# A softmax with quarter rows on each partition, two DMA queues and another order of the vector work

## The chip, the cores and the metric

The kernel runs on one core of a Trainium2 chip. The core has a vector engine (VectorE, DVE in the profile), a scalar engine (ScalarE, ACT), GpSimd (POOL), TensorE (PE, not used here) and SyncE (SP), which only issues DMA transfers and waits. All transfers between the chip's main memory (HBM) and the on-chip memory (SBUF, 128 partitions) run on 16 DMA engines. The metric is the device time of one execution in microseconds; lower is better. Three runs of the kernel before gave 2492.26, 2494.18 and 2495.42 us, so the median is 2494.18 us.

## The reference

The input is `logits`, 16 x 256 x 32768 values of float32, and a temperature of 1.0. Each of the 4096 rows gets a softmax over its 32768 values:

```python
scaled = logits / temperature
scaled = scaled - scaled.max(axis=-1, keepdims=True)
exp_scaled = np.exp(scaled)
return (exp_scaled / exp_scaled.sum(axis=-1, keepdims=True)).astype(np.float32)
```

The input has 536.87 MB and so has the output. Every value is read once and written once.

## The kernel before

A row is cut into two halves of 16384 values, and each half lies on one partition (`_SPLIT = 2`), so two neighbouring partitions hold one row. The 8192 half rows make 64 groups (`G`) of 128 partitions. A group is cut along the row into two chunks of 8192 values (`_CW`, `C = 2`): a chunk is a buffer of 128 x 8192 float32, 32 KB on each partition and 4 MiB in all. There are six such buffers (`_BUFS`), in a pool whose tiles are handed out in turn, and 128 chunks.

For each chunk, `exps` (L94) takes the negative maximum of the chunk on VectorE (L107) and then the exponential in place on ScalarE with that maximum as bias (L114), which adds up the sum of the exponentials as it goes. So each chunk has a maximum of its own. When both chunks of a group are through, `factors` (L123) brings them together: the smaller of the two negative maxima (L129), the same across the two partitions of a row by a shuffle and a combination (`combine`, L84 and L87), the correction of each chunk's maximum (L131, on ScalarE), the corrected sum (L138), again a shuffle and a combination, the reciprocal (L149) and a factor for each chunk (L150). This block has high priority in the scheduler. `scales` (L152) then multiplies a chunk by its factor: the first 4096 values of each partition on VectorE (L160), the other 4096 on ScalarE (L163). In the last group the pieces are 4096 values long.

All transfers are issued on SyncE's queue, loads at L64 and stores at L75, each in the order of the program (`keep_in_program_order`). That order is the list at L170: six loads first, store 0, and from then on store i followed by load i + 5. A load waits until the store that empties its buffer has landed; a store waits for both scaling instructions. The transfers of the first group's loads and of all of the last group are cut into two of 2 MiB. The order of the compute instructions on each engine is left to the scheduler.

Of the kernel before, what the change touches and what calls it, by code (L numbers as in the profile page):

```python
# [6 lines left out]


_SPLIT = 2
_CW = 8192  # L10
_BUFS = 6
_PIECE = 8192
_LAST_DMA = 4096
_DVE_SHARE = 0.5


@with_exitstack
def kernel(
    ctx: ExitStack,
    tc: tile.TileContext,  # L20
    logits: bass.AP,
    temperature: bass.AP,
    out: bass.AP,
):
    nc = tc.nc
    inv_t = 1.0 / float(temperature)
    P = nc.NUM_PARTITIONS
    fp32 = mybir.dt.float32
    Exp = mybir.ActivationFunctionType.Exp
    Copy = mybir.ActivationFunctionType.Copy  # L30
    X = mybir.AxisListType.X
    A = mybir.AluOpType

    xf = logits.flatten_outer_dims()
    of = out.flatten_outer_dims()
    N, V = xf.shape
    W = V // _SPLIT
    CW = min(_CW, W)
    C = W // CW
    assert W * _SPLIT == V and CW * C == W and (N * _SPLIT) % P == 0  # L40
    x = xf.rearrange("n (h v) -> (n h) v", h=_SPLIT)
    o = of.rearrange("n (h v) -> (n h) v", h=_SPLIT)
    G = N * _SPLIT // P
    n_chunks = G * C
    n_rounds = _SPLIT.bit_length() - 1

    xpool = ctx.enter_context(tc.tile_pool(name="x", bufs=_BUFS))
    spool = ctx.enter_context(tc.tile_pool(name="stats", bufs=3))
    slots = {}
    stats = {}  # L50

    def spans(total: int, step: int) -> list[tuple[int, int]]:
        return [(s, min(step, total - s)) for s in range(0, total, step)]

    def piece(g: int) -> int:
        return _PIECE if g < G - 1 else min(_PIECE, _LAST_DMA)

    def load(i: int) -> None:
        g, c = divmod(i, C)
        xs = xpool.tile([P, CW], fp32, tag="x", name="xs")  # L60
        slots[i] = xs
        for s, n in spans(CW, _LAST_DMA if g in (0, G - 1) else CW):
            tc.keep_in_program_order(
                nc.sync.dma_start(  # L64
                    out=xs[:, s : s + n],
                    in_=x[g * P : (g + 1) * P, c * CW + s : c * CW + s + n],
                )
            )

    def store(i: int) -> None:  # L70
        g, c = divmod(i, C)
        xs = slots.pop(i)
        for s, n in spans(CW, _LAST_DMA if g == G - 1 else CW):
            tc.keep_in_program_order(
                nc.sync.dma_start(  # L75
                    out=o[g * P : (g + 1) * P, c * CW + s : c * CW + s + n],
                    in_=xs[:, s : s + n],
                )
            )

    def combine(v, op) -> None:
        for j in range(n_rounds):
            mask = [i ^ (1 << j) for i in range(32)]
            nc.vector.stream_shuffle(  # L84
                out=v[:, j + 1 : j + 2], in_=v[:, j : j + 1], mask=mask
            )
            nc.vector.tensor_tensor(  # L87
                out=v[:, j + 1 : j + 2],
                in0=v[:, j : j + 1],
                in1=v[:, j + 1 : j + 2],  # L90
                op=op,
            )

    def exps(i: int) -> None:  # L94
        g, c = divmod(i, C)
        xs = slots[i]
        ps = spans(CW, piece(g))
        K = C * len(ps)
        if c == 0:
            stats[g] = tuple(  # L100
                spool.tile([P, K], fp32, tag=f"{nm}{K}", name=nm)
                for nm in ("nm", "ssum", "ee", "f", "ttj")
            )
        nm, ssum = stats[g][:2]
        for j, (s, n) in enumerate(ps):
            k = c * len(ps) + j
            nc.vector.tensor_reduce(  # L107
                out=nm[:, k : k + 1], in_=xs[:, s : s + n], axis=X, op=A.max, negate=True
            )
            if inv_t != 1.0:  # L110
                nc.vector.tensor_scalar_mul(
                    out=nm[:, k : k + 1], in0=nm[:, k : k + 1], scalar1=inv_t
                )
            nc.scalar.activation(  # L114
                out=xs[:, s : s + n],
                in_=xs[:, s : s + n],
                func=Exp,
                bias=nm[:, k : k + 1],
                scale=inv_t,
                accum_out=ssum[:, k : k + 1],  # L120
            )

    def factors(g: int) -> None:  # L123
        nm, ssum, ee, f, ttj = stats[g]
        nMh = spool.tile([P, 1 + n_rounds], fp32, tag="nMh", name="nMh")
        Sh = spool.tile([P, 1 + n_rounds], fp32, tag="Sh", name="Sh")
        rS = spool.tile([P, 1], fp32, tag="rS", name="rS")
        with tc.high_priority():
            nc.vector.tensor_reduce(out=nMh[:, 0:1], in_=nm, axis=X, op=A.min)  # L129
            combine(nMh, A.min)  # L130
            nc.scalar.activation(  # L131
                out=ee,
                in_=nm,
                func=Exp,
                bias=nMh[:, n_rounds : n_rounds + 1],
                scale=-1.0,
            )
            nc.vector.tensor_tensor_reduce(  # L138
                out=ttj,
                in0=ee,  # L140
                in1=ssum,
                scale=1.0,
                scalar=0.0,
                op0=A.mult,
                op1=A.add,
                accum_out=Sh[:, 0:1],
            )
            combine(Sh, A.add)
            nc.vector.reciprocal(out=rS, in_=Sh[:, n_rounds : n_rounds + 1])  # L149
            nc.vector.tensor_scalar_mul(out=f, in0=ee, scalar1=rS)  # L150

    def scales(i: int) -> None:  # L152
        g, c = divmod(i, C)
        xs = slots[i]
        f = stats[g][3]
        ps = spans(CW, piece(g))
        for j, (s, n) in enumerate(ps):
            k = c * len(ps) + j
            cut = int(n * _DVE_SHARE) // 512 * 512
            nc.vector.tensor_scalar_mul(  # L160
                out=xs[:, s : s + cut], in0=xs[:, s : s + cut], scalar1=f[:, k : k + 1]
            )
            nc.scalar.activation(  # L163
                out=xs[:, s + cut : s + n],
                in_=xs[:, s + cut : s + n],
                func=Copy,
                scale=f[:, k : k + 1],
            )

    order = [("L", i) for i in range(min(_BUFS, n_chunks))] + [("S", 0)]  # L170
    for i in range(1, n_chunks):
        order.append(("S", i))
        if i + _BUFS - 1 < n_chunks:
            order.append(("L", i + _BUFS - 1))

    nxt = 0
    done = -1
    loaded = 0
    for kind, i in order:
        if kind == "L":  # L180
            load(i)
            loaded = i + 1
        else:
            g = i // C
            if g > done:
                while nxt < (g + 1) * C:
                    assert nxt < loaded
                    exps(nxt)
                    nxt += 1
                factors(g)  # L190
                done = g
            scales(i)
            store(i)


# [33 lines left out]
```

## Time and profile before

| what | value |
|---|---|
| median of three runs | 2494.18 us |
| span of the profiled execution | 2493.8 us |
| VectorE busy | 1487.4 us (60%) |
| ScalarE busy | 1405.0 us (56%) |
| HBM read and written | 536.87 MB each |
| mean rate over the span | 431 GB/s |
| load, issue to landing (4096 KB) | 29.0 us |
| store, issue to landing (4096 KB) | 38.2 us |

The profiled execution has no time of its own beside its span; the span lies 0.4 us under the median of the runs. The page gives the busy time of each engine, the DMA engines' share and rate in slices of the span, the DMA queues, the chain of work that ended last, and the costliest groups of instructions. Such a group is a line of the kernel, an engine and an operation with its shapes; then come the busy time in all, the mean of one in ns, and the idle time of the engine before them with what ended it. A line of a stretch of time gives the stretch, its length, the busy time of DVE, ACT and POOL with their instruction counts, the granted TensorE clock, the share of time that the DMA engines were busy, and GB/s.

### The profile page before, as it was taken

The page shows a single profiled execution, that of the slowest core. Times are in us where ns is not written, and L with a number is a line of the kernel's source. Part 1 is how long each engine was busy: PE and PEld are TensorE (multiplying, and loading weights), DVE is VectorE, ACT ScalarE, POOL GpSimd, SP SyncE. Part 2 cuts the span into 40 slices and gives each one's busy share as a digit, 9 for nine tenths or more (in the row PEclk, how much of TensorE's full clock was granted, in tenths as well). Part 3 has the DMA queues.
Part 4 walks back from the last instruction along what each step waited for, and adds up shares of the span by engine and source line. Part 5 has one row for each costly group of instructions (what it writes and reads, how often), then busy time and mean ns, then how long its engine had stood idle before and what let it go on. Part 6 is the DMA issues. An engine that isn't in the chain of part 4 may idle for free.

```text
span 2493.8 us, 2234 instructions
## 1 busy us (share of the span) xinstructions
DVE 1487.4 (60%) x964; ACT 1405.0 (56%) x455; POOL 0.2 (0%) x4
## 2 busy tenths in 40 slices
DVE  7655565556655566555665566655666566655663
ACT  5665554655556555565555655555546555465553
POOL 0000000000000000000000000000000000000000
DMA  9999999999999999999999999999999999999998
GB/s 412 433 430 432 429 431 432 433 433 434 433 434 432 435 432 435 432 435 431 436 431 435 432 434 433 434 433 433 433 433 433 433 433 434 434 433 434 432 431 368
DMA packets 37745, 1073.90 MB, mean 431 GB/s; under 512 B 4192, under 2 KB 4192, under 8 KB 4192
## 3 DMA queue, kind: packets, MB, share of 16 engines
q1 hardware_dynamic: 37728, 1073.76, 99.9%
q14 instruction: 17, 0.14, 0.0%
HBM read 536.87 MB, written 536.87 MB: 431 GB/s over the span
## 4 chain that ended last, share of the span: by engine, by line
DMA 96%; SPq 1%; ACT 1%; DVE 1%; issue 1%; ACTq 0%
DMA out_dram<-xs 93%; DMA xs<-in_logits_dram 2%; SPq L64 1%; DVE nm L107 1%; ACT xs L163 1%; ACT xs L114 0%; ACTq L224 0%; SPq L75 0%; DVE f L150 0%; ACT ee L131 0%; DVE rS L149 0%; DVE Sh L87 0%; DVE ttj L138 0%; DVE Sh L84 0%; DVE Sh L138 0%
## 5 line engine op out<-in xcount | busy, mean ns | idle before, releaser
L114 ACT ACTIVATE xs<-xs,nm 128x8192 f32<-128x8192 f32 (+1 forms) x130 | 912.1, 7016 | 972.4 <-DVE nm L107 972.4
L107 DVE TENSOR_REDUCE nm<-xs 128x1 f32<-128x8192 f32 (+1 forms) x130 | 1111.6, 8551 | 527.3 <-DMA xs<-in_logits_dram 527.3
L163 ACT ACTIVATE xs<-xs,f 128x4096 f32<-128x4096 f32 (+1 forms) x130 | 468.1, 3648 | 71.4 <-DVE f L150 71.4
L160 DVE TENSOR_SCALAR xs<-xs,f 128x4096 f32<-128x4096 f32 (+1 forms) x130 | 295.7, 2318 | 3.7 <-DVE f L150 1.8
L138 DVE CUSTOM_DVE_ANT_0 ttj<-ee,ssum 128x2 f32<-128x2 f32 x64 | 10.3, 161 | 423.8 <-ACT ee L131 423.8
L114 ACT ACTIVATION_READ_ACCUMULATOR xs<-xs,nm 128x1 f32 x130 | 24.2, 186 | 0.0
L131 ACT ACTIVATE ee<-nm,nMh 128x2 f32<-128x2 f32 x64 | 17.9, 280 | 0.0
L150 DVE TENSOR_SCALAR f<-ee,rS 128x2 f32<-128x2 f32 x64 | 14.6, 229 | 2.2
L149 DVE RECIPROCAL rS<-Sh 128x1 f32<-128x1 f32 x64 | 10.5, 164 | 2.2
L87 DVE TENSOR_TENSOR nMh<-nMh 128x1 f32<-128x1 f32 x64 | 10.2, 160 | 2.2
L87 DVE TENSOR_TENSOR Sh<-Sh 128x1 f32<-128x1 f32 x64 | 10.2, 160 | 2.2
L129 DVE TENSOR_REDUCE nMh<-nm 128x1 f32<-128x2 f32 x64 | 9.9, 155 | 2.2
L84 DVE STREAM_SHUFFLE nMh<-nMh 128x1 f32<-128x1 f32 x64 | 9.7, 151 | 0.0
L84 DVE STREAM_SHUFFLE Sh<-Sh 128x1 f32<-128x1 f32 x64 | 9.7, 151 | 0.0
L114 ACT ACT_TABLE_LOAD x1 | 1.3, 1283 | 12.9 <-DMA xs<-in_logits_dram 12.9
L138 DVE DVE_READ_ACCUMULATOR2_ANT Sh<- 128x1 f32 x64 | 5.3, 84 | 0.0
L84 DVE LOAD_MASK_SELECT Sh<-Sh x64 | 0.9, 14 | 2.8
L84 DVE LOAD_MASK_SELECT nMh<-nMh x64 | 0.9, 14 | 2.7
L210 POOL MEMSET const-bfloat16-1.0<- 128x1 bf16 x1 | 0.1, 102 | 0.0
L210 POOL MEMSET const-uint8-127<- 128x1 uint8 x1 | 0.1, 102 | 0.0
L210 POOL MEMSET const-float32-0.0<- 128x1 f32 x1 | 0.1, 99 | 0.2 <-issue 0.2
L210 POOL MEMSET const-float32-1.0<- 128x1 f32 x1 | 0.1, 99 | 0.0
## 6 DMA issues: line engine op xcount, KB each, us to landing
out_dram<-xs SPq DMA_DIRECT2D x126, 4096.0 KB, 38.2
xs<-in_logits_dram SPq DMA_DIRECT2D x124, 4096.0 KB, 29.0
xs<-in_logits_dram SPq DMA_DIRECT2D x8, 2048.0 KB, 22.3
out_dram<-xs SPq DMA_DIRECT2D x4, 2048.0 KB, 26.7
```

Source lines behind the costliest of these rows:

```text
L64: nc.sync.dma_start(out=xs[:, s : s + n], in_=x[g * P : (g + 1) * P, c * CW + s : c * CW + s + n],)
L84: nc.vector.stream_shuffle(out=v[:, j + 1 : j + 2], in_=v[:, j : j + 1], mask=mask)
L87: nc.vector.tensor_tensor(out=v[:, j + 1 : j + 2], in0=v[:, j : j + 1], in1=v[:, j + 1 : j + 2], op=op,)
L107: nc.vector.tensor_reduce(out=nm[:, k : k + 1], in_=xs[:, s : s + n], axis=X, op=A.max, negate=True)
L114: nc.scalar.activation(out=xs[:, s : s + n], in_=xs[:, s : s + n], func=Exp, bias=nm[:, k : k + 1], scale=inv_t, accum_out=ssum[:, k : k + 1],
L129: nc.vector.tensor_reduce(out=nMh[:, 0:1], in_=nm, axis=X, op=A.min)
L131: nc.scalar.activation(out=ee, in_=nm, func=Exp, bias=nMh[:, n_rounds : n_rounds + 1], scale=-1.0,)
L138: nc.vector.tensor_tensor_reduce(out=ttj, in0=ee, in1=ssum, scale=1.0, scalar=0.0, op0=A.mult, op1=A.add, accum_out=Sh[:, 0:1],)
L149: nc.vector.reciprocal(out=rS, in_=Sh[:, n_rounds : n_rounds + 1])
L150: nc.vector.tensor_scalar_mul(out=f, in0=ee, scalar1=rS)
L160: nc.vector.tensor_scalar_mul(out=xs[:, s : s + cut], in0=xs[:, s : s + cut], scalar1=f[:, k : k + 1])
L163: nc.scalar.activation(out=xs[:, s + cut : s + n], in_=xs[:, s + cut : s + n], func=Copy, scale=f[:, k : k + 1],)
```

## The change

A row is now cut into quarters (`_SPLIT = 4`), so four neighbouring partitions hold one row and a tile of 128 x 8192 float32 holds 32 whole rows. There is one tile per group and there are 128 groups; the chunks and their separate maxima are gone. The tile is 4 MiB and lies in one piece in HBM. Six fixed buffers of 32 KB per partition are used in turn, and four sets of small tiles.

`peaks` takes the negative maximum of the tile and combines it across the four partitions in two rounds of shuffle and combination. `exps` then uses the maximum of the whole row as bias, so no correction is needed. `scales` combines the sums in two rounds, takes the reciprocal and multiplies the whole tile on VectorE; ScalarE no longer scales. Loads are issued on SyncE's queue; stores are issued on ScalarE's queue, but for the last two tiles, whose stores are on SyncE's. The order on every engine is that of the program (`manual_schedule`): the maximum and the exponential of tile i + 1 stand before the scaling and the store of tile i, and load i + 6 comes after store i. Tile 0 and tile 127 are loaded and worked on in two halves of 4096 values, and tile 127 is stored in two halves.

```diff
-_SPLIT = 2
-_CW = 8192
+_SPLIT = 4
 _BUFS = 6
-_PIECE = 8192
-_LAST_DMA = 4096
-_DVE_SHARE = 0.5
+_END_CUT = 4096
...
+    pool = ctx.enter_context(tc.tile_pool(name="fixed", bufs=1))
+    bufs = [pool.tile([P, W], fp32, name=f"x{b}") for b in range(_BUFS)]
...
+    def cuts(i: int) -> list[tuple[int, int]]:
+        step = _END_CUT if i in (0, G - 1) else W
+        return [(s, step) for s in range(0, W, step)]
 
     def load(i: int) -> None:
...
+        xs = bufs[i % _BUFS]
+        for s, n in cuts(i):
+            nc.sync.dma_start(
+                out=xs[:, s : s + n], in_=x[i * P : (i + 1) * P, s : s + n]
             )
 
+    def store(i: int, eng) -> None:
+        xs = bufs[i % _BUFS]
+        for s, n in cuts(i) if i == G - 1 else [(0, W)]:
+            eng.dma_start(out=o[i * P : (i + 1) * P, s : s + n], in_=xs[:, s : s + n])
...
+    def peaks(i: int) -> None:
...
+        for (s, n), t in zip(cs, to):
+            nc.vector.tensor_reduce(
+                out=t, in_=xs[:, s : s + n], axis=X, op=A.max, negate=True
+            )
+        if len(cs) > 1:
+            nc.vector.tensor_reduce(
+                out=mx[:, 0:1], in_=pk[:, : len(cs)], axis=X, op=A.min
+            )
+        combine(mx, A.min)
...
     def exps(i: int) -> None:
...
+        for (s, n), t in zip(cs, to):
             nc.scalar.activation(
                 out=xs[:, s : s + n],
                 in_=xs[:, s : s + n],
                 func=Exp,
-                bias=nm[:, k : k + 1],
+                bias=mx[:, R : R + 1],
                 scale=inv_t,
-                accum_out=ssum[:, k : k + 1],
+                accum_out=t,
             )
...
+    def scales(i: int) -> None:
...
+        combine(su, A.add)
+        nc.vector.reciprocal(out=rs, in_=su[:, R : R + 1])
+        for s, n in cs:
             nc.vector.tensor_scalar_mul(
-                out=xs[:, s : s + cut], in0=xs[:, s : s + cut], scalar1=f[:, k : k + 1]
-            )
-            nc.scalar.activation(
-                out=xs[:, s + cut : s + n],
-                in_=xs[:, s + cut : s + n],
-                func=Copy,
-                scale=f[:, k : k + 1],
+                out=xs[:, s : s + n], in0=xs[:, s : s + n], scalar1=rs
             )
...
+    with tc.manual_schedule():
+        for i in range(_BUFS):
             load(i)
+        peaks(0)
+        exps(0)
+        for i in range(G):
+            if i + 1 < G:
+                peaks(i + 1)
+                exps(i + 1)
+            scales(i)
+            store(i, nc.scalar if i < G - 2 else nc.sync)
+            if i + _BUFS < G:
+                load(i + _BUFS)
```

More of the change, by code (lines that the diff above doesn't have):

```diff
@@ L29 @@
     Exp = mybir.ActivationFunctionType.Exp
-    Copy = mybir.ActivationFunctionType.Copy
     X = mybir.AxisListType.X
@@ L37 @@
     W = V // _SPLIT
-    CW = min(_CW, W)
-    C = W // CW
-    assert W * _SPLIT == V and CW * C == W and (N * _SPLIT) % P == 0
+    assert W * _SPLIT == V and (N * _SPLIT) % P == 0
     x = xf.rearrange("n (h v) -> (n h) v", h=_SPLIT)
@@ L43 @@
     G = N * _SPLIT // P
[L44 to L56, printed above, removed]
-    def load(i: int) -> None:
[L59 to L66, printed above, removed]
-                )
-            )
@@ L70, in store @@
[L70 to L79, printed above, removed]
+    R = _SPLIT.bit_length() - 1
+    pool = ctx.enter_context(tc.tile_pool(name="fixed", bufs=1))
+    bufs = [pool.tile([P, W], fp32, name=f"x{b}") for b in range(_BUFS)]
@@ new lines @@
+    stats = [
+        (
+            pool.tile([P, 4], fp32, name=f"pk{b}"),
+            pool.tile([P, 4], fp32, name=f"sm{b}"),
+            pool.tile([P, R + 1], fp32, name=f"mx{b}"),
+            pool.tile([P, R + 1], fp32, name=f"su{b}"),
+            pool.tile([P, 1], fp32, name=f"rs{b}"),
+        )
+        for b in range(4)
+    ]
+    def cuts(i: int) -> list[tuple[int, int]]:
+        step = _END_CUT if i in (0, G - 1) else W
+        return [(s, step) for s in range(0, W, step)]
+    def load(i: int) -> None:
+        xs = bufs[i % _BUFS]
+        for s, n in cuts(i):
+            nc.sync.dma_start(
+                out=xs[:, s : s + n], in_=x[i * P : (i + 1) * P, s : s + n]
+            )
@@ L81, in combine @@
+    def store(i: int, eng) -> None:
+        xs = bufs[i % _BUFS]
+        for s, n in cuts(i) if i == G - 1 else [(0, W)]:
+            eng.dma_start(out=o[i * P : (i + 1) * P, s : s + n], in_=xs[:, s : s + n])
     def combine(v, op) -> None:
-        for j in range(n_rounds):
-            mask = [i ^ (1 << j) for i in range(32)]
+        for j in range(R):
+            mask = [k ^ (1 << j) for k in range(32)]
             nc.vector.stream_shuffle(
@@ L92, in combine @@
             )
-    def exps(i: int) -> None:
[L95 to L113, printed above, removed]
+    def peaks(i: int) -> None:
+        xs = bufs[i % _BUFS]
+        pk, _, mx, _, _ = stats[i % 4]
+        cs = cuts(i)
+        to = [mx[:, 0:1]] if len(cs) == 1 else [pk[:, k : k + 1] for k in range(len(cs))]
+        for (s, n), t in zip(cs, to):
[5 more added lines that the diff above has]
+                out=mx[:, 0:1], in_=pk[:, : len(cs)], axis=X, op=A.min
+            )
+        combine(mx, A.min)
+        if inv_t != 1.0:
+            nc.vector.tensor_scalar_mul(
+                out=mx[:, R : R + 1], in0=mx[:, R : R + 1], scalar1=inv_t
+            )
+    def exps(i: int) -> None:
+        xs = bufs[i % _BUFS]
+        _, sm, mx, su, _ = stats[i % 4]
+        cs = cuts(i)
+        to = [su[:, 0:1]] if len(cs) == 1 else [sm[:, k : k + 1] for k in range(len(cs))]
+        for (s, n), t in zip(cs, to):
             nc.scalar.activation(
@@ L117, in exps @@
                 func=Exp,
-                bias=nm[:, k : k + 1],
+                bias=mx[:, R : R + 1],
                 scale=inv_t,
-                accum_out=ssum[:, k : k + 1],
+                accum_out=t,
             )
[L123 to L130, printed above, removed]
-            nc.scalar.activation(
[L132 to L136, printed above, removed]
-            )
[L138 to L146, printed above, removed]
-            )
-            combine(Sh, A.add)
-            nc.vector.reciprocal(out=rS, in_=Sh[:, n_rounds : n_rounds + 1])
-            nc.vector.tensor_scalar_mul(out=f, in0=ee, scalar1=rS)
@@ L152, in scales @@
[L152 to L160, printed above, removed]
-                out=xs[:, s : s + cut], in0=xs[:, s : s + cut], scalar1=f[:, k : k + 1]
-            )
-            nc.scalar.activation(
-                out=xs[:, s + cut : s + n],
-                in_=xs[:, s + cut : s + n],
-                func=Copy,
-                scale=f[:, k : k + 1],
-            )
@@ L170 @@
[L170 to L180, printed above, removed]
-            load(i)
[L182 to L191, printed above, removed]
+    def scales(i: int) -> None:
+        xs = bufs[i % _BUFS]
+        _, sm, _, su, rs = stats[i % 4]
+        cs = cuts(i)
+        if len(cs) > 1:
+            nc.vector.tensor_reduce(
+                out=su[:, 0:1], in_=sm[:, : len(cs)], axis=X, op=A.add
+            )
+        combine(su, A.add)
+        nc.vector.reciprocal(out=rs, in_=su[:, R : R + 1])
+        for s, n in cs:
+            nc.vector.tensor_scalar_mul(
+                out=xs[:, s : s + n], in0=xs[:, s : s + n], scalar1=rs
+            )
@@ L192 @@
+    with tc.manual_schedule():
+        for i in range(_BUFS):
+            load(i)
+        peaks(0)
[4 more added lines that the diff above has]
+                exps(i + 1)
             scales(i)
-            store(i)
+            store(i, nc.scalar if i < G - 2 else nc.sync)
+            if i + _BUFS < G:
+                load(i + _BUFS)
 _INS = ['logits', 'temperature']
```

## The prediction

> **What bounds the kernel now.** I read the page's engine shares first, then the DMA queues, then the chain, then the queue engine's own waits.
>
> ```profile
> span 2493.8 us, 2234 instructions
> DVE 1487.4 (60%) x964; ACT 1405.0 (56%) x455; POOL 0.2 (0%) x4
> ...
> q1 hardware_dynamic: 37728, 1073.76, 99.9%
> ...
> DMA 96%; SPq 1%; ACT 1%; DVE 1%; issue 1%; ACTq 0%
> ```
>
> No compute engine passes 60%; the 16 DMA engines are busy 99.9% of the span on one queue, and 96% of the chain is DMA. The waits of SyncE's queue say how work stays in front of them:
>
> ```profile
> SPq L64 <- DMA out_dram<-xs: 2246.9, 122, 19.6
> ```
>
> Each load (L64) waits for a store to free its buffer, and there are still some four transfers in the queue behind it. Stretches of the span, with DMA share and GB/s in the last two columns:
>
> ```profile
> 60.00:65.00 5.00, 4.89 (x7) 3.36 (x4) 0.00 (x0) 1.00 0.83 347
> ...
> 700.00:1700.00 1000.00, 601.88 (x390) 564.27 (x181) 0.00 (x0) 1.00 1.00 433
> ...
> 2480.00:2483.00 3.00, 0.00 (x0) 0.00 (x0) 0.00 (x0) 1.00 0.83 355
> 2483.00:2486.00 3.00, 0.00 (x0) 0.00 (x0) 0.00 (x0) 1.00 0.46 197
> 2486.00:2489.00 3.00, 0.00 (x0) 0.00 (x0) 0.00 (x0) 1.00 0.15 66
> 2489.00:2493.80 4.80, 0.00 (x0) 0.00 (x0) 0.00 (x0) 1.00 0.04 17
> ```
>
> The middle runs at a flat 433 GB/s. The end is ragged: from 2480 the share falls because some engines are done and others are not. The busy time there is 3 x (0.83 + 0.46 + 0.15) + 4.8 x 0.04 = 4.5 of 13.8 us, so 9.3 us go to unequal engines and the last completion. That is nearly all that is not line rate: 1073.76 MB at 433 GB/s are 2479.8 us, 14.0 below the span. So the question is what the change does to the rate, the two ends and the raggedness. The rows for compute:
>
> ```profile
> L107 DVE TENSOR_REDUCE nm<-xs 128x1 f32<-128x8192 f32 x126 | 1094.0, 8682 | 523.4 <-DMA xs<-in_logits_dram 523.4
> L114 ACT ACTIVATE xs<-xs,nm 128x8192 f32<-128x8192 f32 x126 | 897.2, 7121 | 965.1 <-DVE nm L107 965.1
> L163 ACT ACTIVATE xs<-xs,f 128x4096 f32<-128x4096 f32 x126 | 460.4, 3701 | 70.3 <-DVE f L150 70.3
> L160 DVE TENSOR_SCALAR xs<-xs,f 128x4096 f32<-128x4096 f32 x126 | 290.8, 2350 | 3.7 <-DVE f L150 1.8
> ```
>
> **Part by part.** A tile is 4 MiB in and 4 MiB out both before and after: 8.389 MB at 433 GB/s, a period of 19.4 us.
>
> *Compute.* VectorE per tile: the maximum 8.68, two shuffle and combine pairs for it (4 small instructions, which follow each other every 0.19 us in the rows: 0.76), the same for the sum with the reciprocal (0.95), and all of the scaling (2 x 2.35 = 4.70): 15.1 us. Before it was 1487.4 / 128 = 11.6. ScalarE: 7.12 + 0.19 and a store issue; an issue takes 0.33 to 0.39 us on SyncE's queue, so 7.7 us, against 1405.0 / 128 = 11.0 before. Both stay under 19.4 and are costed at nothing while the DMA queues hold work. The cover is VectorE's 4.3 us spare per tile; past that each us more would cost 128 us.
>
> *Moved order and its waits.* VectorE now takes the maximum of tile i+1 before scaling tile i, so scaling i waits for load i+1. ScalarE issues store i behind the exponential of i+1 and holds at it until scaling i ends; only the exponential of i+2 is behind it, which needs a maximum VectorE starts later anyway, so nothing more waits. SyncE holds load i+6 until store i has landed; behind it are only later loads. Is one buffer's round shorter than 6 x 19.4 = 116 us? From its landing: load i+1 up to 19.4 later, its maximum 9.4, its exponential 7.3, store issue 0.4 (scaling i, 5.7, runs beside the exponential): 36.5. The store at half of the bandwidth takes 19.4, with one store ahead of it up to 38.8: 75. That leaves 41 us for a load that needs 19.4 at half bandwidth, so the load queue holds about two loads and the engines do not run dry. Steady state: 0.
>
> *Two queues.* Bytes, 32 KB packets per partition row, and number of transfers (259 against 262) are as before, so the unknown is what an engine pays to alternate between loads and stores packet by packet instead of every 8 packets (128 partitions over 16 engines). The middle stretch bounds it:
>
> ```profile
> DMA packets 26035, 758.03 MB, mean 433 GB/s; under 512 B 2893, under 2 KB 2893, under 8 KB 2893
> ...
> q14 instruction: 12, 0.10, 0.0%
> ```
>
> These are 500 to 2250 us: 26035 - 2893 - 12 = 23130 data packets, one per engine every 16 x 1750 / 23130 = 1.2105 us. In the packet records consecutive starts on one engine are most often 1.209 us apart. The excess, 1.5 ns per packet or 12 ns per group of 8, holds the completion packet and any price of a change of direction. Paid at each of 2096 packets instead of 262 it is at most 1834 x 12 ns = 22 us. From below: two 16 KB packets start 0.607 apart each, so a packet has a fixed part of 2 x 0.607 - 1.209 = 5 ns; hidden behind the other queue at all 2096, that is -10 us. I take 0: only 2% of the 32 KB packets last over 1.213 us although one in eight follows a change of direction. The change of pitch from 64 to 32 KB has no row of its own; I count it inside these ends.
>
> *Opening.* First data 1.8 us into the span as before. Store 0 goes earlier than the 51.9 us of before: the maximum of tile 0 in two halves from 8 us on, that of tile 1 from its landing at 22.7 (then 8.7 + 0.8), its exponential to 39.6, then the store. Six loads keep the engines busy until 60. The weak 60 to 65 us stretch (347) is followed by 446, 452 and 459, packets counted later, so filling it brings under 1 us: 0.
>
> *Tail.* Let T be the landing of the last half load. Then maximum 4.4, small work 1.0, closing tile 126's sum 0.95 and scaling it 4.7, issue and start 1.1: store 126 moves at T + 12.1. Before that only what is left of store 125 can fill the engines. Tile 126 landed earlier; 17.2 us later (8.7 + 0.8 + 7.3 + 0.4) store 125 was issued. If the queues take turns by packet, 16 KB halves against 32 KB rows get a third, so the last load takes 29 us and store 125 was issued at T - 11.8. With no store ahead of it, 11.8 x 2/3 = 7.9 of its 9.7 us are done at T and the gap is 12.1 - 1.8 = 10.3. With a full one ahead, 9.7 remain and the gap is 2.4. With equal bytes the load ends sooner, more store work is left, and it is 0. VectorE starts with loaded tiles in hand, so the first stores come every 15.1 us to a queue that serves one in 19.4; this leaves nearly a store waiting, and nothing later works it off. I take 3, with 0 and 10 as ends. The old tail had no such gap (429 GB/s at 2470 to 2480).
>
> The page "DMA: Bandwidth & Descriptors" of the Trainium skill (section "Queues, rings and completion order") lets an engine drain a whole packet of 9 to 17 descriptors from one queue before it turns; a half load's 8 rows would then be one turn, again a third of the bytes, and 2497.4 in all; equal bytes would give 2494.4. No row shows two loaded queues. Its section "Where 436 GB/s comes from" has a ceiling of 435.2 GB/s, by which the bytes need 2467.3 us; the measured 433 leaves 12 us to it, an estimate of the most that any queueing could bring (2485 in all).
>
> *Instruction fetch.* VectorE runs 11 instructions per tile (maximum, 4, 4, reciprocal, scaling) in place of 13 per pair, 576 more in all. The whole fetch queue moved 17 packets, 0.14 MB; half as much again is 0.07 MB, 0.2 us.
>
> **Sum:** 2493.8 + 0 (rate) + 0 (opening) + 3 (tail) + 0.2 = 2497.0 of span. The median of the three runs is 2494.18, 0.4 above the profiled span, so 2497.4 us.
>
> **Rivals.**
>
> *A, the turns cost (slower).* Each engine pays something at each change of direction: the bound is 22 us, half is 11. For it: the 12 ns are there. Against: the completion packet alone is recorded with 9 ns. It decides from 2 us on, 1 ns per packet, since with the tail the time is then over 2499.2. Half the price gives 2508.
>
> *B, faster.* Either the 5 ns are hidden by the other queue (-10), or the engines end more nearly together, and of the 9.3 us at the ragged end 8 come back. One of them with the tail gap: 2497.4 - 10 = 2487. For it: reads and writes of the engines mix all the time, so no common phase builds up. Against: the load-only stretch from 10 to 50 us (438 GB/s, uncertain by some 13 for packets cut at its edges) is no proof of a faster line, and the raggedness arises while queues are full, which they stay.
>
> *C, the change does nothing that shows.* Tail gap 0: 2494.4, inside the forecast.
>
> *D, starvation.* VectorE's 15.1 stretches over 19.4 while two queues use the SBUF. Nothing shows it: the maximum takes 8.68 at 99.9% DMA. At 20 us per tile, 0.6 over the period, it would be 2494 + 128 x 0.6 = 2571.
>
> **How the numbers follow.** A change under 0.2% (5.0 us, 2489.2 to 2499.2) cannot be told from none. Forecast with C: 0.47. A: 0.31, D: 0.02, so slower 0.33. B: 0.20. The range reaches to half of B and to over half of A, and leaves out some 0.2: 2487 to 2509. The forecast's own range is 2493 to 2499.
>
> **What would show it.** Right: q1 split into two queues of 537 MB each with shares that sum near 99.9%, 433 GB/s in the middle, VectorE near 15.1 x 128 = 1930 us (77%), ScalarE near 940, and a dip of 2 to 4 us of DMA share some 25 us before the end. A is right if the middle falls to 428 to 431 with a full share; B if it rises to 434 or 435, or the ragged end shortens to 2 us; D if VectorE passes 95%. Wrong altogether if the DMA share of the middle is under 0.97: then the round of a buffer is longer than my 75 us and the load queue runs dry.

## The result and the profile after

The changed kernel takes 2501.62 us (median of 6 runs, 2500.96 to 2502.86). The kernel before, run beside it, took 2494.8 us (6 runs, 2492.26 to 2495.84). The ratio is 1.0029 with a 95% interval of 1.0018 to 1.0041: slower by 0.3%, some 7 us. The profiled execution has a span of 2499.8 us and a time of 2501.61, so 1.8 us lie around the span.

The page of the changed kernel, its span, engines, DMA queues and chain:

```profile
span 2499.8 us, 2866 instructions
DVE 1857.8 (74%) x1928; ACT 925.3 (37%) x261; POOL 0.2 (0%) x4
...
q1 hardware_dynamic: 19152, 545.27, 50.6%
q10 hardware_dynamic: 18144, 528.49, 49.0%
q14 instruction: 22, 0.18, 0.0%
...
DMA 83%; DVE 15%; ACT 1%; issue 0%; DVEq 0%; SPq 0%; ACTq 0%
```

The work is now split between two queues, whose shares sum to 99.6%. VectorE runs 1928 instructions where there were 964 (the mask loads of the shuffles count), and the queue that fetches instructions moved 22 packets where there were 17.

Stretches of the changed kernel (length, busy DVE, ACT and POOL, TensorE clock, DMA share, GB/s):

```profile
700.00:1700.00 1000.00, 742.58 (x767) 370.39 (x104) 0.00 (x0) 1.00 1.00 433
...
2450.00:2460.00 10.00, 7.23 (x2) 4.82 (x2) 0.00 (x0) 1.00 0.99 426
2460.00:2465.00 5.00, 0.00 (x0) 0.00 (x0) 0.00 (x0) 1.00 0.60 259
2465.00:2470.00 5.00, 2.87 (x1) 0.00 (x0) 0.00 (x0) 1.00 0.09 39
2470.00:2475.00 5.00, 4.63 (x16) 2.44 (x1) 0.00 (x0) 1.00 0.06 26
2475.00:2480.00 5.00, 2.90 (x1) 5.00 (x4) 0.00 (x0) 1.00 0.34 144
2480.00:2490.00 10.00, 5.56 (x10) 0.05 (x1) 0.00 (x0) 1.00 1.00 429
```

The middle is what it was: 433 GB/s at a full share. All of the loss shows at the end. From 2464 us most DMA engines stand still, and from 2468 to 2479 us all but one: a share of 0.06 is one engine of 16. Before, the engines also ended unequally, but at the very last transfer.

The timeline of the changed kernel there (start, length, engine, line, operation, and the wait before it):

```profile
2452.81 4.41 DVE L88 TENSOR_REDUCE pk<-x 128x1 f32<-128x4096 f32 x1
...
2467.14 4.42 DVE L88 TENSOR_REDUCE pk<-x 128x1 f32<-128x4096 f32 x1 [9.91 <-DMA x<-in_logits_dram]
...
2473.41 4.49 DVE L127 TENSOR_SCALAR x<-x,rs 128x8192 f32<-128x8192 f32 x1
...
2477.93 8.29 SPq L67 DMA_DIRECT2D out_dram<-x  x3
```

VectorE waits 9.9 us for the second half of the last tile until 2467.1. The share of the engines says that most of them had finished this load long before; it waits for one late engine. Then come the maximum, the scaling of tile 126 and, at 2477.9, its store.

How late that engine is can be followed through the whole run. Each of the 16 DMA engines reports the end of its part of a transfer. This table, from the trace's records of these reports, has the distance from the first to the last of the 16 in us (with two queues it swings by up to 1.6 between a load and a store; the table takes the one that is nearest in time):

```
time in the span, us    180   526   875  1223  1571  1920  2268  2435
kernel before           1.4   6.5   7.2   7.8   8.4   9.1   9.8  10.5
changed kernel          1.5   4.9   7.6   9.4  11.1  12.9  14.6  14.9
```

In the kernel before most of it comes between 180 and 500 us, and then steps of 0.6 to 0.8 us follow at 447, 758, 1068, 1379, 1689, 2000 and 2310 us. In the changed kernel it rises to the end by 0.9 to 1.0 us at a time, at 213, 388, 544, 719, 875, 1050, 1206, 1381 us and so on. At each of these times an 8 KB packet of the instruction queue starts. That made the theory for the experiments, F: VectorE's instructions are fetched 8 KB at a time through one DMA engine, and at each fetch this engine falls behind the others by nearly 1 us. If each engine has 8 of the 128 partition rows of every transfer, it has as many bytes to move as every other, and the last store waits for it. The trace does not name the engine of a packet; that these fetches fall on one engine is read from the latest report alone moving at each of them.

The packet records show where the time goes. A 32 KB packet of the changed kernel usually takes 1.21 us. From 100 us on only 21 take over 1.3 us, and each of them starts as the packet of a fetch ends. Behind the fetches at the times above they take 1.75 to 1.83 us, behind the others 1.45 to 1.63. So one of those fetches costs its engine its own 0.31 us and 0.54 to 0.62 us of the packet behind it, 0.89 on average. In the kernel before, the packet behind such a fetch takes 1.57 or 1.58 us, which makes 0.67. Why that packet takes longer no run shows.

### The profile page after: what moved, and what is told of

Read it like the earlier page. It is cut to its first block, busy times and chain, and to the rows that moved or that the text cites. A ratio compares the mean times of both kernels' runs of the same rounds, so it can differ in the third digit from the quotient of the medians.

```text
span 2499.8 us, 2866 instructions
## 1 busy us (share of the span) xinstructions
DVE 1857.8 (74%) x1928; ACT 925.3 (37%) x261; POOL 0.2 (0%) x4
## 4 chain that ended last, share of the span: by engine, by line
DMA 83%; DVE 15%; ACT 1%; issue 0%; DVEq 0%; SPq 0%; ACTq 0%
DMA out_dram<-x 43%; DMA x<-in_logits_dram 40%; DVE mx L88 9%; DVE x L127 4%; ACT x L107 1%; DVE mx L72 0%; DVE su L75 0%; DVE su L72 0%; DVE mx L75 0%; DVE pk L88 0%; DVE rs L125 0%; DVEq L174 0%; SPq L60 0%; DVE su L121 0%; DVE mx L92 0%
## 5 line engine op out<-in xcount | busy, mean ns | idle before, releaser
L88 DVE TENSOR_REDUCE mx<-x 128x1 f32<-128x8192 f32 x126 | 1094.4, 8686 | 564.1 <-DMA x<-in_logits_dram 564.1
L107 ACT ACTIVATE x<-x,mx 128x8192 f32<-128x8192 f32 (+1 forms) x130 | 912.2, 7017 | 1546.5 <-DVE su L72 1469.8
L127 DVE TENSOR_SCALAR x<-x,rs 128x8192 f32<-128x8192 f32 (+1 forms) x130 | 574.5, 4421 | 4.5
L75 DVE TENSOR_TENSOR su<-su 128x1 f32<-128x1 f32 x256 | 40.9, 160 | 8.8
L75 DVE TENSOR_TENSOR mx<-mx 128x1 f32<-128x1 f32 x256 | 40.9, 160 | 8.8
L72 DVE STREAM_SHUFFLE su<-su 128x1 f32<-128x1 f32 x256 | 38.8, 151 | 0.0
L72 DVE STREAM_SHUFFLE mx<-mx 128x1 f32<-128x1 f32 x256 | 38.8, 151 | 0.0
L88 DVE TENSOR_REDUCE pk<-x 128x1 f32<-128x4096 f32 x4 | 17.7, 4418 | 18.5 <-DMA x<-in_logits_dram 18.5
L125 DVE RECIPROCAL rs<-su 128x1 f32<-128x1 f32 x128 | 21.0, 164 | 4.5
L107 ACT ACTIVATION_READ_ACCUMULATOR x<-x,mx 128x1 f32 x130 | 24.2, 186 | 0.0
```

What stands on the lines that cost most here:

```text
L72: nc.vector.stream_shuffle(out=v[:, j + 1 : j + 2], in_=v[:, j : j + 1], mask=mask)
L75: nc.vector.tensor_tensor(out=v[:, j + 1 : j + 2], in0=v[:, j : j + 1], in1=v[:, j + 1 : j + 2], op=op,)
L88: nc.vector.tensor_reduce(out=t, in_=xs[:, s : s + n], axis=X, op=A.max, negate=True)
L107: nc.scalar.activation(out=xs[:, s : s + n], in_=xs[:, s : s + n], func=Exp, bias=mx[:, R : R + 1], scale=inv_t, accum_out=t,)
L125: nc.vector.reciprocal(out=rs, in_=su[:, R : R + 1])
L127: nc.vector.tensor_scalar_mul(out=xs[:, s : s + n], in0=xs[:, s : s + n], scalar1=rs)
```

## The experiments

Three things were to be told apart: the fetches (F) against a DMA engine that is slow for another reason; what the second queue does; and the gap at the end. The times of the kernel before beside these runs were 2494.1 to 2495.0 us. The last table of the lateness, after the runs, has all of them.

**One queue.** All stores on SyncE's queue:

```diff
-            store(i, nc.scalar if i < G - 2 else nc.sync)
-            if i + _BUFS < G:
-                load(i + _BUFS)
+            store(i, nc.sync)
+            if i >= 1 and i + _BUFS - 1 < G:
+                load(i + _BUFS - 1)
```

> The changed kernel with all stores on SyncE's queue, load i + 5 after store i as in the kernel before. Reading Q (the uneven DMA engines of the kernel before, five or more of them 4 to 6 us late by 450 us, come from loads and stores alternating in one queue): the same lateness appears here, and the time rises by up to 5 us over the changed kernel's 2501.6. Reading P (it comes from the 64 KB pitch of the half rows in HBM): no such lateness, since the tile is still in one piece, and the time stays within 2 us of 2501.6. Both expect 433 GB/s in the middle; if two queues cost rate, this kernel is faster by over 5 us.

Measured: 2501.52 us (6 runs; ratio to before 1.0033, 1.0021 to 1.0045), the same as with two queues. The middle has 433 GB/s here too, so two queues neither cost nor bring rate. The last engine was 15.6 us late at the end. The four next to it were 2.5 to 3.4 us late at 526 us, between the two readings. The page "DMA: Bandwidth & Descriptors" of the Trainium skill says the same in its section "Issuing engines are not separate DMA queues": issuing from several engines only saves the time of issuing. The two rates agree with it. That the two times, 2501.52 and 2501.62 us, agree so closely is partly chance: with one queue the late engine reports without a gap to the end, and in return it is 15.6 us late there and not 12.9.

**The kernel before with its stores on ScalarE's queue.**

```diff
                tc.keep_in_program_order(
-                nc.sync.dma_start(
+                nc.scalar.dma_start(
                     out=o[g * P : (g + 1) * P, c * CW + s : c * CW + s + n],
```

> The kernel before with its stores on ScalarE's queue and nothing else. Reading Q: the early lateness of the DMA engines (4 to 6 us by 450 us) goes, the last engine is then about 5 us late at the end from its instruction fetches alone, and the time falls from 2494.5 to 2489 or 2490. Reading P: the lateness stays, time within 2 us of 2494.5. If a store in ScalarE's queue holds up its exponentials until the DMA engines run dry, the DMA share of the middle falls under 0.99 and the time rises.

Measured: 2924.27 us, ratio 1.1728 (1.1709 to 1.1748): the last case. One stretch and two of ScalarE's waits in this run:

```profile
1000.00:2000.00 1000.00, 509.11 (x330) 472.14 (x153) 0.00 (x0) 1.00 0.87 365
```

```profile
ACT xs L163 <- DVE f L150: 1045.6, 62, 17.6
ACT ee L131 <- DVE nMh L87: 419.3, 63, 21.4
```

The DMA engines are busy 0.87 of the time. ScalarE stands at the scaling (L163) for up to 17.6 us, with the store behind it, and the loads wait for the store. The scheduler also put ScalarE's other work in another order, so the run says nothing about the early lateness, and how much of its loss is the queue and how much the order was not separated.

**More instructions on VectorE.** Ten tiny writes per tile that nothing uses:

```diff
...
             scales(i)
+            for k in range(10):
+                nc.vector.memset(junk[:, k : k + 1], 0.0)
             store(i, nc.scalar if i < G - 2 else nc.sync)
```

> The changed kernel with ten more tiny writes by VectorE per tile, 1280 instructions in all, in its spare time. Theory F (every 128 instructions of VectorE are an 8 KB fetch on one and the same DMA engine, which falls 0.95 us behind at each): ten more fetches, the last engine 9 to 10 us later, time 2510 to 2511. Rival R (that DMA engine is slow for a reason that has nothing to do with instructions): 2501.6, within 2 us, because VectorE has over 4 us per tile to spare.

Measured: 2517.06 us (4 runs, 2511.01 to 2519.3; ratio 1.0090, 1.0075 to 1.0105), 15.4 us over the changed kernel. The page of this run:

```profile
DVE 1874.7 (75%) x3208; ACT 925.3 (37%) x261; POOL 0.2 (0%) x4
...
DMA  9999999999999999999999999999999999999995
GB/s 413 433 432 433 433 433 434 433 433 432 433 433 431 432 433 433 433 433 432 433 433 434 433 433 433 433 433 433 433 433 433 434 433 433 433 433 427 411 418 253
...
q14 instruction: 32, 0.26, 0.0%
```

1280 instructions and 17 us of VectorE time, ten fetches, and the end moves by 15 us though VectorE is still idle a quarter of the time. The rival falls. The expected size was too small, and not because a fetch came to cost more. Until 1746 us seven more fetches had made 6.1 us more lateness (18.1 against 12.0), as expected, and the packet behind each of VectorE's fetches takes 1.74 to 1.86 us from 100 us to the end. From 1920 to 2290 us the late engine's reports come 19.35 us apart for each tile, and 1 us more at a fetch. The eight tiles after that take it 163.8 us, which is 9.0 more than 8 x 19.35, with only two fetches in them. There many other packets last longer too: of the 32 KB packets that start from 2300 to 2400 us, 83 take over 1.3 us, against 1 to 3 in each 100 us from 100 to 2200. The page has 411 and 418 GB/s in these slices, at a DMA share of 0.99 and 1.00. So some 7 of the 15.4 us are no price of a fetch; what slows the packets once the engine is over 20 us behind was not found.

**The same on GpSimd.**

```diff
...
             scales(i)
+            nc.gpsimd.tensor_copy(out=junk[:, 15:16], in_=stats[i % 4][4])
+            for k in range(9):
+                nc.gpsimd.memset(junk[:, k : k + 1], 0.0)
             store(i, nc.scalar if i < G - 2 else nc.sync)
```

> The changed kernel with the ten additional tiny instructions per tile on GpSimd, not on VectorE. If each engine's instructions are fetched through a DMA engine of its own, GpSimd's engine falls some 10 us behind and stays ahead of VectorE's (13 to 15 us), and the time is 2501.6 to 2503. If all fetches go through the same DMA engine, or any fetch delays all engines: about 2517 as with ten on VectorE.

Measured: 2501.96 us (5 runs; ratio 1.0034, 1.0021 to 1.0046), no change. Its page:

```profile
DVE 1858.0 (74%) x1928; ACT 925.3 (37%) x261; POOL 598.7 (24%) x1284
...
q14 instruction: 34, 0.28, 0.0%
```

There are more fetches in all than with the ten on VectorE (34 against 32), and they cost nothing. The second latest engine was 8.3 us late at the end against 5.8 in the changed kernel, the latest 14.6 as before. This fits that it is not the number of fetches that counts but how many fall on the latest engine, and that GpSimd's do not fall on VectorE's.

**The tail.** Scaling and store of tile 126 ahead of the work on tile 127:

```diff
-            if i + 1 < G:
+            if i + 1 < G - 1:
                 peaks(i + 1)
                 exps(i + 1)
             scales(i)
             store(i, nc.scalar if i < G - 2 else nc.sync)
+            if i + 1 == G - 1:
+                peaks(i + 1)
+                exps(i + 1)
```

> The changed kernel with scaling and store of tile 126 put ahead of the maximum and exponential of tile 127. If the late DMA engine really stands idle for the 2.4 us read from its landings (2477.2 to 2479.6), and this gap belongs to the late store 126, the time falls by 2 to 3 us to 2499. Rival: the other 13 engines' long wait from 2463 on is what counts, then up to 12 us are won (2490). If the late engine decides all and has no gap: 2501.6.

Measured: 2498.4 us (10 runs, 2498.05 to 2500.33; ratio 1.0017, 1.0008 to 1.0027), 3.2 us less. The first case holds. Stretches of this run:

```profile
2475.00:2480.00 5.00, 0.00 (x0) 5.00 (x3) 0.00 (x0) 1.00 0.09 39
2480.00:2485.00 5.00, 3.98 (x10) 0.76 (x2) 0.00 (x0) 1.00 0.06 26
```

The other engines still stand still for some 10 us, and that costs nothing: the late engine's packets now follow each other without a gap. Its last packet of store 126 ends at 2485.53 us, and its first of the next store starts at 2485.54; on the other engines that store had begun at 2485.2, just in time.

**Fewer instructions on VectorE.** The sum over the four partitions by a matmul with a matrix of ones in blocks of four, on top of the mended tail:

```diff
...
-        combine(su, A.add)
-        nc.vector.reciprocal(out=rs, in_=su[:, R : R + 1])
+        nc.tensor.matmul(tot[i % 4], same, su[:, 0:1], start=True, stop=True)
+        nc.vector.reciprocal(out=rs, in_=tot[i % 4])
```

> The run with the mended tail, and the sum across the four partitions made by one small matmul on TensorE in place of two shuffle and combination rounds (six of VectorE's 15 instructions per tile with the mask loads). Theory F (each 128 instructions of VectorE cost the late DMA engine 0.95 us): 768 instructions fewer are 6 fetches fewer, 2498.4 - 5.7 = 2492.7, within 2. If the number of VectorE's instructions doesn't matter: 2498.4. If the way through TensorE is so much longer that stores come late: over 2500, with a DMA share under 0.99 in the middle.

Measured: 2494.31 us (11 runs; ratio 1.0004, 0.9996 to 1.0013), 4.1 us less than with the tail alone, and level with the kernel before. Theory F had 2492.7 within 2. The last engine was 10.1 us late against 13.6.

**Fewer still.** The bias from a second matmul. It is then the mean of the row's four quarter maxima and no longer the row's maximum:

```diff
-        combine(mx, A.min)
+        nc.tensor.matmul(mid[i % 4], mean, mx[:, 0:1], start=True, stop=True)
...
+        nc.scalar.activation(
+            out=mx[:, R : R + 1], in_=mid[i % 4], func=mybir.ActivationFunctionType.Copy,
+            scale=inv_t,
+        )
...
```

> The run with the sum on TensorE, and as bias of the exponential the mean of a row's four quarter maxima, made by a second small matmul and copied by ScalarE, in place of the row's maximum; it is the same softmax as long as a quarter's maximum lies less than some 80 above that mean. VectorE keeps 3 instructions per tile out of 9. Theory F: 768 instructions fewer are 6 fetches fewer on VectorE's DMA engine, which would end 5.7 us earlier; the next DMA engine is by then 6 to 7 us late itself (against 9.5 to 10 of the late one), so 3 to 4 us are won: 2490 to 2491, faster than both kernels by 0.15%. If the fetches were not it: 2494.3.

Measured: 2491.41 us (11 runs, 2491.09 to 2491.64; ratio 0.9986, 0.9977 to 0.9995), 2.9 us less again and faster than both kernels, a little above the 2490 to 2491 of theory F. Its page:

```profile
span 2489.7 us, 2623 instructions
...
PE 130.0 (5%) x512; PEld 118.9 (5%) x512; DVE 1708.3 (69%) x392; ACT 947.2 (38%) x389; POOL 2.5 (0%) x10
...
q14 instruction: 12, 0.10, 0.0%
```

VectorE is down to 392 instructions, and the last engine is 6.1 us late. In the two steps its lateness fell by 3.5 and 4.0 us and the time by 4.1 and 2.9; how much of this the other work at the very end does was not separated.

**The pitch in HBM.** To see where the early lateness of the kernel before comes from, tiles were made of every other quarter row, so that their partitions lie 64 KB apart. This run and the next leave out that a row's quarters belong together, so what they compute is not the softmax:

```diff
+    xp = xf.rearrange("n (a b v) -> (n a) b v", b=2, v=W)
+    op = of.rearrange("n (a b v) -> (n a) b v", b=2, v=W)
+
+    def rows(t, i: int):
+        g, c = divmod(i, 2)
+        return t[g * P : (g + 1) * P, c]
...
-                out=xs[:, s : s + n], in_=x[i * P : (i + 1) * P, s : s + n]
+                out=xs[:, s : s + n], in_=rows(xp, i)[:, s : s + n]
...
```

> The changed kernel with every tile made of every other quarter row, so that the partitions of a tile lie 64 KB apart in HBM as in the kernel before and not 32 KB; a row's four quarters are then in two tiles and the combination across partitions joins the wrong ones, so this computes something else than the softmax, with the same work. Reading P (the early lateness of five or more DMA engines in the kernel before comes from the pitch): it appears here, 4 to 6 us by 450 us, time 2501.6 to 2506. Reading Q: it doesn't, 2501.6 within 2.

Measured: 2502.36 us (4 runs; ratio 1.0035, 1.0021 to 1.0048), and at 526 us the five latest engines stood at 1.7, 1.7, 1.8, 1.9 and 2.8 us. The pitch alone is not it.

With one queue on top of that:

> The same with all stores on SyncE's queue, so both the pitch and the single queue of the kernel before; it too leaves the rows joined wrongly. If pitch and queue together make the early lateness: five or more DMA engines 4 to 6 us late by 450 us. With the pitch alone as cause the same as in the run with two queues. If neither makes it, at most the 3.4 us of the run with one queue and 32 KB.

Measured: 2501.73 us (9 runs, seven of them from 2501.35 to 2502.05, the others 2504.61 and 2523.53; ratio 1.0044, 1.0026 to 1.0063). The five latest at 526 us: 2.6, 2.7, 4.2, 4.4 and 6.0, against 4.0, 4.1, 4.2, 6.0 and 6.5 in the kernel before and 2.5, 2.5, 3.3, 3.4 and 5.4 with one queue and 32 KB. The three runs with one queue have more early lateness than those with two; the kernel before has the most, and what adds the rest stays open.

The lateness of the last of the 16 engines in all runs but the one of 2924 us, as in the first table. In the run with ten more on VectorE the two last values are of stores; the loads beside them are 21.2 and 23.8 us late.

```
time in the span, us    180   526   875  1223  1571  1920  2268  2435   time, us
kernel before           1.4   6.5   7.2   7.8   8.4   9.1   9.8  10.5   2494.8
changed kernel          1.5   4.9   7.6   9.4  11.1  12.9  14.6  14.9   2501.6
one queue               3.1   5.4   8.2   9.9  11.4  13.1  14.8  15.6   2501.5
ten more on VectorE     1.9   7.2   9.9  13.5  16.2  19.9  27.5  28.3   2517.1
ten more on GpSimd      1.3   4.0   5.7   7.5   9.2  11.9  13.7  14.6   2502.0
64 KB pitch             2.4   2.8   5.5   7.3   9.0  10.8  12.5  13.4   2502.4
64 KB, one queue        2.5   6.0   8.7  10.4  11.9  13.6  15.3  16.1   2501.7
mended tail             2.3   3.0   5.7   7.5   9.2  11.0  12.7  13.6   2498.4
and sum on TensorE      1.8   3.8   5.6   6.4   7.2   9.0   9.9  10.1   2494.3
and bias on TensorE     0.5   1.7   2.5   3.3   3.9   4.7   5.9   6.1   2491.4
```

## Why the prediction was right or wrong

The time lies inside the stated range, but above the forecast's own range of 2493 to 2499, and the change is slower by more than the 0.2% that I called no change, to which I gave 0.47. The 0.33 for slower were placed on another mechanism, a price for each turn, and the range reached so far up for its sake. That the time lies inside it is luck. Step by step:

- **Rate, two queues (0): right.** 433 GB/s before and after, and the run with one queue has the same time. Rival A is not what made it slower; it would have shown in the middle.
- **Compute (0): right.** VectorE has 1857.8 / 128 = 14.5 us per tile against 15.1 reckoned (the scaling in one piece takes 4.49, not 4.70) and ScalarE 925 against 940. VectorE waits 564 us in all for loads, so rival D did not come up.
- **Opening (0): right.** Store 0 is issued at 37.9 us, and the first slice of the span has 411 GB/s where it had 412.
- **Tail (3): right in place and nearly in size.** Store 126 was issued 10.8 us after the last half load, against 11.0 reckoned. By the packet records the late engine ends store 125 at 2476.35, and store 126 starts on all engines at 2478.8: a gap of 2.4 us, and mending the tail brought 3.2. The last load took 29.1 us (2438.06 to 2467.14, the starts of VectorE's maxima that waited for it and for the load before) against 29 reckoned from a third of the bytes. The turns of several rows that the prediction took from the Trainium skill (page "DMA: Bandwidth & Descriptors", section "Queues, rings and completion order") would give the same third, but the packet records do not show them: on the late engine a 16 KB row of the load starts at 2463.02, a 32 KB row of the store at 2463.63, a load row at 2464.84 and a store row at 2465.45, so a turn is one row here. What I had not seen is that the gap is to be read on the late engine; the other engines wait some 15 us and it doesn't matter.
- **Instruction fetch (0.2): this is the step that failed.** I spread 0.07 MB more over 16 engines at line rate. The packets do not spread: VectorE's all fall on one engine, and each costs it 0.6 to 1.0 us, two to three times the 0.309 us that such a packet itself takes in the trace; the rest is the longer packet behind it. The count was short too: I had 576 more instructions on VectorE, and the pages have 964 more, because the mask loads count. Within the span the kernel before has 8 of VectorE's fetches and the changed one 15, and that engine ends the run. Shown from both sides: 1280 more instructions on VectorE cost 15.4 us (some 7 of them by another way, as said), 768 fewer brought 4.1 and 768 fewer again 2.9.
- **Raggedness (kept as it is): right in sum and wrong in its parts.** Taken at the loads of the changed kernel, to keep one kind of transfer, the last engine is 3.3 us late at 508 us and 13.9 at 2405. Over 14 fetches from 178 us on (1.5 late) that is 12.4 / 14 = 0.89 us each. In the kernel before it rises from 6.5 at 526 to 10.5 at 2434 over 6 fetches, 0.67 each. So the fetches make 15 x 0.89 = 13.3 instead of 8 x 0.67 = 5.4 us, 8 more, and what is left of the early part is 3.3 - 3 x 0.89 = 0.6 instead of 6.5 - 2 x 0.67 = 5.2, 4.6 less. By this sum the change would have cost over 10 us without this part, which I had not seen either. What made the early part smaller stays open.
- **The sum, as the reports give it.** The first engine ends at 2482.4 us in the kernel before. In the changed one it ends store 125 at 2463.5, and with the two last stores (20.0 us, from 2478.8 to the last report at 2498.8) it would have ended at 2483.5 without the gap: 1.1 later. The last engine is 12.9 us behind it at store 125 in place of 10.5 at the end: 2.4. The gap is 2.4. Together 5.9 us; the spans differ by 2499.8 - 2493.8 = 6.0.
- **Span to time (0.4): off.** I took the median of before as 0.4 us above the span of its profile. A run's time is 1.8 above its own span (2501.61 against 2499.8); the profiled execution of the kernel before was simply one of the longer ones. So 1.4 of the 4.2 us between forecast and result are this, and 2.8 are in the span.

The arithmetic that made the small term look safe was a mean: the page has the instruction queue at 0.0% of 16 engines. What counts is the engine that is last, and the ragged end, which I showed and took as given, was its mark.

## What to carry to other kernels

In a kernel bound by DMA, look at the last microseconds of the DMA share: if they fall off in steps, one engine sets the end, and a mean over the engines hides what it is doing. There, many small instructions on one compute engine cost time even when that engine is idle a quarter of the span, and moving a few of them to an engine whose fetches fall elsewhere brings it back. A last tile's own work should stand behind the store of the tile before it.

## What the runs showed of the hardware

- In the kernels without matmuls instructions are fetched 8 KB at a time, about one fetch to 130 executed instructions (2866 and 22, 2234 and 17, 4146 and 32). VectorE's fetches delay one DMA engine by steps of 0.6 to 0.8 us each in the kernel before and 0.9 to 1.0 in the changed one, which shrink a little until the next; GpSimd's delay another. The greater part is not the fetch's own 0.31 us but the 32 KB packet behind it, which takes 1.57 or 1.58 and 1.75 to 1.83 us in place of 1.21.
- With both queues loaded, an engine alternates between loads and stores row by row at no measurable cost: 433 GB/s with one queue and with two.
- The latest engine can be 15 us behind the first with the middle still at 433 GB/s. In the run in which it was 21 us behind and more from 2260 us on, the last slices fell to 427, 411, 418 and 253 GB/s; in the first three the DMA share was still 0.99 to 1.00, so the packets took longer there and the engines did not run dry.
